# One kernel, a list of new due times, one scaling moved from GpSimd to ScalarE, and three slots with queues of their own

## The chip, the cores and the metric

The kernel runs on one core of a Trainium2 chip. Its engines are TensorE (PE, with its weight loads as PEld), VectorE (DVE), ScalarE (ACT), GpSimd (POOL) and SyncE (SP, which here issues DMAs). The metric is the device time of one execution in microseconds; lower is better.

## The reference

An encoder layer is applied to two sequences, x_prompt and x_sample, each 1024 positions of 1024 features; everything is fp32, and d_ff is 4096. Cut to what matters here:

```
h    = rmsnorm(x, g_mix); proj = h @ w_in
oa   = diff_attention(...)     # 4 heads: softmax 0 minus lam * softmax 1, then @ v
ob   = dilated_mixture(...)    # 8 heads, three patterns of (window, dilation):
                               #   (128,1), (512,4), (2048,16)
  for each pattern: s = q k^T * scale - slope * dist, softmax in the window, o = p @ v, lse
  out  = sum_i softmax_i(lse_i) * o_i
x    = x + concat(norm(oa), norm(ob)) @ w_out
x    = x + square(relu(rmsnorm(x, g_mlp) @ w_up)) @ w_down
y    = rmsnorm(x, g_final)
```

The weights of a dilated head's patterns, softmax over the patterns' denominators, become one factor for each row of probabilities; the kernel multiplies the probabilities by it before they meet v. It joins the three patterns into two sets of scores: bands (dilation 1) and classes (positions with the same remainder modulo 4).

## The kernel before

Each fp32 operand of a large product is split into a rounded high part and the rest, a low part, and three products hi*hi, hi*lo and lo*hi are summed on TensorE. The high part is a cast, mostly on ACT, the low part a subtraction on DVE or POOL. So nearly every product on PE stands behind a pair cast, subtraction.

The work is 16 attention units (8 per sequence; even numbers are two dilated heads, odd ones two differential heads in four tasks), the output projection, and the MLP, whose up and down products use a scheme with 7 instead of 8 block products: it needs sums of weight blocks (`s1` to `s4` in `mlp_up`).

A dilated head m of unit n has two spans. In `a{n}.{m}` (`dil_a`) PE makes 8 blocks of band scores `p1` (128x192 or 128x256) and 8 blocks of class scores `p2` (128x256). DVE adds the bias with a running minimum, ACT takes the exponential. Then the denominators are exchanged between the two layouts by a small permutation product on PE (`cross`, operand `perm`): DVE masks the result into a tile of tag `e`, and reduces it to the factors `dd` (bands) and `f2` (classes). Eight instructions scale `p1` by `dd` and eight scale `p2` by `f2`, all on POOL. In `b{n}.{m}` (`dil_b`) the helper `parts` transposes four 128x128 pieces of the probabilities into PSUM on PE, ACT casts them to the high part (`CAST wt<-psb`), DVE subtracts the low part, and PE multiplies both with v into `pss`. The output goes to a tile `x` of tag `big`.

No loop issues the instructions directly. All work is first recorded into a `Plan`. A table `KEYS` gives each span a start and an end (in units of roughly one attention unit), from which each instruction gets a due time. `Plan.order` then goes through a model of the five engines with its own costs, and on every engine takes the ready instruction that is due first and whose slots are free. Operations with alternatives (`ALT_SUB`, `ALT_MUL`, `ALT_ADD`) go to POOL or DVE, whichever takes them first. `emit` (line 450) issues in that order, so each engine runs a fixed list, in order, and every row of the trace reads L450: rows are told apart by tiles.

Tiles come from tags with a number of slots: `wt` 5 halves of 128x512, `big` 8 of 128x1024, `q` 12. A tag has queues (lanes): within one queue slots are handed out strictly in the order of due times, so a tile that is due earlier and not yet wanted holds up a later one. The changed lines are `q_into` and `k_into` (the scaled q and k before their split, tag `wt`), `dil_a` (the two scalings) and `dil_b` (the tile `x`).

Of the kernel before, what the change touches and what calls it, by code (L numbers as in the profile page):

```python
# [12 lines left out]
F32 = mybir.dt.float32  # L13
# [3 lines left out]
AF = mybir.ActivationFunctionType  # L17
# [29 lines left out]
    "u0": (-4.872, 0.128), "lam": (1.273, 1.359), "a0.0": (0.318, 0.491), "b0.0": (0.695, 0.818),  # L47
    "a0.1": (0.564, 0.959), "b0.1": (0.907, 1.356), "u1": (-0.336, 0.921), "a1.0": (1.16, 1.17),
    "b1.0": (1.384, 1.394), "a1.1": (1.217, 1.476), "b1.1": (1.482, 1.492), "a1.2": (1.521, 2.068),
    "b1.2": (2.062, 2.072), "a1.3": (0.842, 1.209), "b1.3": (1.568, 2.056), "ro1": (2.198, 2.709),  # L50
    "u2": (1.08, 1.998), "a2.0": (1.83, 1.892), "b2.0": (2.698, 2.732), "a2.1": (2.322, 3.199),
    "b2.1": (3.083, 3.202), "u3": (2.615, 2.859), "a3.0": (3.01, 3.22), "b3.0": (3.495, 3.505),
    "a3.1": (3.363, 3.373), "b3.1": (4.079, 4.089), "a3.2": (3.601, 3.727), "b3.2": (4.243, 4.253),
    "a3.3": (3.845, 3.931), "b3.3": (4.137, 4.169), "r1": (2.29, 3.154), "ro3": (3.208, 5.313),
    "u4": (2.996, 3.936), "a4.0": (4.3, 4.31), "b4.0": (4.326, 4.358), "a4.1": (4.269, 5.245),
    "b4.1": (5.263, 5.273), "u5": (4.35, 5.123), "a5.0": (4.877, 5.092), "b5.0": (5.599, 5.609),
    "a5.1": (4.761, 5.876), "b5.1": (5.92, 5.948), "a5.2": (5.207, 5.761), "b5.2": (5.997, 6.117),
    "a5.3": (5.692, 6.054), "b5.3": (6.231, 6.241), "ro5": (6.971, 8.003), "u6": (5.116, 5.981),
    "a6.0": (6.121, 6.131), "b6.0": (6.468, 6.505), "a6.1": (6.434, 6.444), "b6.1": (6.908, 7.14),
    "rg0": (7.977, 8.031), "u7": (5.779, 7.117), "a7.0": (7.1, 7.11), "b7.0": (7.121, 7.486),  # L60
    "a7.1": (7.231, 7.529), "b7.1": (7.554, 7.564), "a7.2": (7.848, 7.912), "b7.2": (8.264, 8.274),
    "a7.3": (7.419, 7.863), "b7.3": (7.608, 8.726), "ro7": (8.492, 8.976), "x": (6.498, 7.176),
    "u8": (7.315, 8.152), "a8.0": (7.997, 8.766), "b8.0": (8.442, 8.775), "a8.1": (8.373, 8.913),
    "b8.1": (9.208, 9.431), "u9": (8.465, 9.183), "a9.0": (8.719, 8.845), "b9.0": (9.936, 9.946),
    "a9.1": (9.591, 10.219), "b9.1": (10.364, 10.437), "a9.2": (8.775, 8.951), "b9.2": (9.497, 9.507),
    "a9.3": (9.562, 9.725), "b9.3": (10.146, 10.156), "ro9": (8.751, 10.698), "u10": (9.24, 10.203),
    "a10.0": (10.545, 10.597), "b10.0": (10.454, 11.086), "a10.1": (10.633, 10.935), "b10.1": (11.156, 11.166),
    "u11": (10.001, 11.039), "a11.0": (10.988, 10.998), "b11.0": (11.337, 12.024), "a11.1": (11.405, 11.602),
    "b11.1": (11.559, 11.916), "a11.2": (12.015, 12.078), "b11.2": (12.033, 12.059), "a11.3": (11.566, 11.916),
    "b11.3": (11.973, 12.339), "ro11": (11.81, 12.373), "u12": (11.182, 11.192), "a12.0": (12.369, 12.493),  # L70
    "b12.0": (12.486, 13.117), "a12.1": (12.219, 12.881), "b12.1": (13.193, 13.415), "u13": (12.244, 12.871),
    "a13.0": (13.077, 13.375), "b13.0": (13.654, 13.692), "a13.1": (13.411, 13.421), "b13.1": (13.693, 13.703),
    "a13.2": (13.806, 13.864), "b13.2": (14.036, 14.124), "a13.3": (13.913, 13.923), "b13.3": (14.122, 14.313),
    "ro13": (13.424, 13.484), "u14": (13.268, 13.612), "a14.0": (14.014, 14.058), "b14.0": (14.617, 14.93),
    "a14.1": (14.123, 14.668), "b14.1": (14.892, 15.12), "rg1": (15.833, 15.876), "u15": (14.405, 15.268),
    "mix": (14.668, 16.212), "a15.0": (15.131, 15.677), "b15.0": (15.493, 16.435), "a15.1": (15.218, 15.531),
    "b15.1": (15.321, 15.634), "a15.2": (15.514, 15.947), "b15.2": (15.799, 16.683), "a15.3": (16.152, 16.411),
    "b15.3": (16.539, 16.638), "ro15": (16.018, 16.028), "out0.0": (15.43, 16.237), "out0.1": (16.478, 17.321),
    "mix0": (16.801, 16.811), "out1.0": (17.313, 17.799), "mix1": (16.996, 17.37), "out1.1": (17.873, 18.085),
    "in0": (17.372, 18.332), "up0.0": (19.76, 19.97), "up0.1": (19.108, 19.877), "as0": (17.468, 19.18),  # L80
    "up0.2": (18.279, 18.585), "up0.3": (19.951, 20.229), "as1": (19.497, 19.731), "up0.4": (20.258, 20.341),
    "up0.5": (20.208, 20.256), "as2": (20.161, 21.47), "up0.6": (22.325, 22.655), "up0.7": (20.453, 22.109),
    "as3": (21.899, 23.125), "up0.8": (22.556, 22.913), "up0.9": (24.937, 25.048), "as4": (20.662, 22.037),
    "up0.10": (23.998, 24.008), "up0.11": (23.047, 23.405), "as5": (22.537, 24.004), "up0.12": (25.576, 25.586),
# [1411 lines left out]
```

## Time and profile before

| | us |
|---|---|
| median of 3 runs | 2608.33 (2605.42 to 2615.72) |
| profiled execution, own time | 2610.55 |
| its span | 2608.4 |
| PE busy | 2523.4 (97%) |
| DVE busy | 1961.3 (75%) |
| ACT busy | 1408.4 (54%) |
| POOL busy | 760.6 (29%) |

Attention takes the span's first 1048 us or so, the output projection's end and the first MLP up product follow at about 1310 us, and the down products end the span. The profile page gives busy time by engine, a coarse picture in 40 slices, the DMA queues, the chain of work that ended last, and groups of instructions by tile. In a timeline row the first number is the start in us from the span's start, the second the length; a bracket says how long the engine had stood idle before and who released it. A row with "x8" is eight instructions back to back.

### The profile page before, as it was taken

The page shows a single profiled execution, that of the slowest core. Times are in us where ns is not written, and L with a number is a line of the kernel's source. Part 1 is how long each engine was busy: PE and PEld are TensorE (multiplying, and loading weights), DVE is VectorE, ACT ScalarE, POOL GpSimd, SP SyncE. Part 2 cuts the span into 40 slices and gives each one's busy share as a digit, 9 for nine tenths or more (in the row PEclk, how much of TensorE's full clock was granted, in tenths as well). Part 3 has the DMA queues.
Part 4 walks back from the last instruction along what each step waited for, and adds up shares of the span by engine and source line. Part 5 has one row for each costly group of instructions (what it writes and reads, how often), then busy time and mean ns, then how long its engine had stood idle before and what let it go on. Part 6 is the DMA issues. An engine that isn't in the chain of part 4 may idle for free. (4 is left out here: it accounts for less than half of the span.)

```text
span 2608.4 us, 36729 instructions
## 1 busy us (share of the span) xinstructions
PE 2523.4 (97%) x12482; PEld 2102.5 (81%) x12482; DVE 1961.3 (75%) x3593; ACT 1408.4 (54%) x2659; POOL 760.6 (29%) x642
## 2 busy tenths in 40 slices
PE   8999999999999999999989999999999999999997
PEld 6888888878888888777777888878887788888877
DVE  7778877897868788887987777557689777545677
ACT  5666665876565757644444444533446545443334
POOL 2305122331223121444342222113243211122464
PEclk9999999999999999999999999999999999999998
DMA  4123121432212121466767666869845444665541
GB/s 163 56 73 112 53 72 47 126 105 67 59 55 75 51 66 56 146 230 220 272 212 256 227 224 231 304 211 357 295 154 177 175 165 136 242 235 198 206 154 65
DMA packets 181402, 412.42 MB, mean 158 GB/s; under 512 B 21344, under 2 KB 27872, under 8 KB 181216
## 3 DMA queue, kind: packets, MB, share of 16 engines
q1 hardware_dynamic: 180640, 409.95, 46.2%
q8 instruction: 98, 1.61, 0.2%
q14 instruction: 88, 0.72, 0.1%
q10 hardware_dynamic: 576, 0.15, 0.0%
HBM read 285.76 MB, written 107.48 MB: 151 GB/s over the span
## 5 line engine op out<-in xcount | busy, mean ns | idle before, releaser
L450 PE MATMUL psb<-h,w 128*128 128x512 f32 x4512 | 1183.7, 400 | 20.0 <-ACT h L450 8.5
L450 PEld LDWEIGHTS psb<-h,w 128*128 128x128 f32 x4512 | 829.0, 190 | 189.7 <-ACT h L450 9.5
L450 PE MATMUL psb<-h 128*128 128x512 f32 (+1 forms) x2448 | 569.9, 383 | 5.3 <-DVE q L450 4.0
L450 PEld LDWEIGHTS psb<-h 128*128 128x128 f32 x2448 | 446.3, 189 | 97.2 <-DVE q L450 2.9
L450 POOL TENSOR_TENSOR w<-w 128x512 fp32r<-128x512 f32 (+1 forms) x127 | 175.0, 1383 | 785.4 <-ACT w L450 659.1
L450 ACT CAST h<-big 128x1024 fp32r<-128x1024 f32 x218 | 220.3, 1051 | 306.2 <-PE psb L450 167.8
L450 DVE TENSOR_TENSOR wt<-psb,wt 128x512 fp32r<-128x512 f32 (+2 forms) x448 | 282.4, 647 | 122.0 <-ACT wt L450 81.0
L450 DVE TENSOR_TENSOR h<-big,h 128x1024 fp32r<-128x1024 f32 x153 | 219.6, 1457 | 125.2 <-ACT h L450 111.5
L450 POOL TENSOR_TENSOR h<-big,h 128x1024 fp32r<-128x1024 f32 x65 | 165.6, 2560 | 384.4 <-ACT h L450 285.6
L450 ACT CAST w<-w 128x512 fp32r<-128x512 f32 x262 | 157.5, 617 | 184.6 <-DMA w<-w_up 95.5
L450 DVE TENSOR_TENSOR w<-w 128x512 fp32r<-128x512 f32 (+1 forms) x233 | 193.7, 836 | 62.1 <-ACT w L450 50.1
L450 PE MATMUL psb<-big,w 128*128 128x512 f32 x768 | 230.2, 394 | 7.1 <-ACT wt L450 7.1
L450 ACT CAST wt<-psb 128x512 fp32r<-128x512 f32 (+2 forms) x288 | 147.6, 538 | 150.1 <-PE psb L450 137.5
L450 PE MATMUL pss<-k,q 128*128 128x512 f32 (+2 forms) x768 | 207.9, 370 | 10.5 <-DVE k L450 4.9
L450 ACT ACTIVATE big<-big,nm 128x1024 f32<-128x1024 f32 x128 | 147.5, 1153 | 66.7 <-DVE nm L450 65.1
L450 PEld LDWEIGHTS psb<-big,w 128*128 128x128 f32 x768 | 145.2, 189 | 39.6 <-ACT wt L450 8.5
L450 PE MATMUL psb<-ident,big 128*128 128x128 f32 (+1 forms) x1032 | 166.2, 273 | 3.2 <-DVE v L450 1.2
L450 DVE CUSTOM_DVE_ANT_0 big<-pss,strip_a 128x1024 f32<-128x1024 f32 x128 | 154.8, 1216 | 10.4 <-PE pss L450 8.6
L450 PEld LDWEIGHTS pss<-k,q 128*128 128x128 f32 x768 | 128.6, 192 | 35.5 <-DVE nm L450 10.4
L450 ACT ACTIVATE wt<-wt 128x512 f32<-128x512 f32 x224 | 133.3, 627 | 37.2 <-DVE wt L450 35.2
L450 ACT ACTIVATE big<-big,s 128x256 f32<-128x256 f32 (+1 forms) x256 | 125.8, 494 | 40.3 <-DVE s L450 40.0
L450 PEld LDWEIGHTS psb<-ident,big 128*128 128x128 f32 (+1 forms) x1032 | 124.0, 140 | 18.5 <-issue 1.6
(184 smaller groups left out, 3429.6 us busy)
## 6 DMA issues: line engine op xcount, KB each, us to landing
ad<-wt SPq DMA_DIRECT2D x218, 256.0 KB, 2.9
big<-ad SPq DMA_DIRECT2D x109, 512.0 KB, 4.5
big<-sd SPq DMA_DIRECT2D x60, 512.0 KB, 4.8
w<-w_in SPq DMA_DIRECT2D x102, 256.0 KB, 3.0
big<-w_down SPq DMA_DIRECT2D x49, 512.0 KB, 4.9
w<-w_up SPq DMA_DIRECT2D x96, 256.0 KB, 4.2
q<-q SPq DMA_DIRECT2D x128, 128.0 KB, 2.3
q<-od SPq DMA_DIRECT2D x64, 256.0 KB, 3.6
```

The source lines that it names most:

```text
L450: getattr(getattr(self.nc, e), m)(**{k: x(v) for k, v in op.kw.items()})
```

## The change

Four edits. The third is on the engine that does it, the second and fourth on which queue a slot is taken from, the first on the order of everything:

```
 KEYS = {                      # all retuned: 198 of 203 pairs have other numbers, for instance
-    "a6.1": (6.434, 6.444), "b6.1": (6.908, 7.14),
+    "a6.1": (6.707, 6.717), "b6.1": (6.933, 6.943),
-    "up0.2": (18.279, 18.585),
+    "up0.2": (18.217, 19.115),
...
     def q_into(q, r):
...
-            t = half("wt")
+            t = half("wt", F32, "e")
...
         k.extend(full("k", F32R) for _ in range(2))
         def evac(_, hf, pb):
-            t = half("wt")
+            t = half("wt", F32, "e")
...
         for b in range(NB):
-            POOL.tensor_scalar(out=p2[b], in0=p2[b], scalar1=f2[:, b // 2, b % 2:b % 2 + 1], scalar2=1.0,
-                               op0=ALU.mult, op1=ALU.mult)
+            ACT.activation(out=p2[b], in_=p2[b], func=AF.Identity, scale=f2[:, b // 2, b % 2:b % 2 + 1])
...
     def dil_b(u, m):
...
-        x = full("big")
+        x = full("big", F32, "x")
```

Over the whole program the issue lists keep PE at 12452 instructions and move the other engines a little: DVE 3595 to 3592, ACT 2281 to 2409, POOL 647 to 522. The 128 instructions from POOL to ACT are 16 heads of 8 scalings. PE rows that carry a wait go from 2249 to 2179; in attention, from 1532 to 1445.

Two places, in the issue lists. The first is the second dilated head of unit u6. On POOL the band scalings (by `dd`) and class scalings (by `f2`) of that head stand in a row before:

```order
L450 TENSOR_SCALAR big_5345<-big_5345,dd_5686 128x192 [waits DVE_49,Activation_49]
L450 TENSOR_SCALAR big_5345<-big_5345,dd_5686 128x256 x3
L450 TENSOR_SCALAR big_5363<-big_5363,dd_5686 128x256 x3
L450 TENSOR_SCALAR big_5363<-big_5363,dd_5686 128x192
L450 TENSOR_SCALAR big_5505<-big_5505,f2_5785 128x256 [waits DVE_49,Pool_49]
L450 TENSOR_SCALAR big_5505<-big_5505,f2_5785 128x256 x3
L450 TENSOR_SCALAR big_5562<-big_5562,f2_5785 128x256 [waits Pool_49]
L450 TENSOR_SCALAR big_5562<-big_5562,f2_5785 128x256 x3
L450 TENSOR_TENSOR q_5432<-q_5432,q_5842 128x512 [waits DMAHW1_49,Activation_49]
```

The class scalings are rows 5 to 8 of these; the next POOL instruction is a norm's product for q. After the change they stand on ACT:

```order
L450 CAST k_5090<-wt_5783 64x512 [waits DVE_49]
L450 ACTIVATE h_5790<-w_5766,g_76 128x512 [waits DMAHW0_49]
L450 ACTIVATE h_5799<-w_5775,g_76 128x512 [waits DMAHW1_49]
L450 CAST k_5091<-wt_5783 64x512
L450 CAST wt_5794<-psb_5793 128x512 [waits PE_49]
L450 ACTIVATE q_5779<-q_5779 128x512 [waits DMAHW2_49]
L450 ACTIVATE big_5589<-big_5589,f2_5834 128x256 [waits DVE_49]
L450 ACTIVATE big_5589<-big_5589,f2_5834 128x256 x3
L450 ACTIVATE big_5615<-big_5615,f2_5834 128x256 x4
L450 CAST wt_5813<-psb_5812 128x512 [waits PE_49,Activation_49]
L450 ACTIVATE h_5863<-w_5824,g_76 128x512 [waits DMAHW3_49]
L450 ACTIVATE big_5663,l0_5869<-big_5663,nm_5857 128x1024 [waits DVE_49]
```

The last of the eight is directly in front of `CAST wt_5813<-psb_5812`, a high part of that head's transposed probabilities. On PE this part of the list reads, after the change:

```order
L450 MATMUL psb_5820<-e_5810,perm1_74 128x32 [waits DVE_49]
L450 MATMUL psb_5812<-ident_68,big_5543 128x128 [waits Pool_49]
L450 MATMUL pss_5662<-k_5090,q_4990 128x512 [waits DVE_49,Activation_49]
L450 MATMUL pss_5662<-k_5090,q_4991 128x512
L450 MATMUL pss_5802<-k_5090,q_4990 128x512
L450 MATMUL pss_5802<-k_5090,q_4991 128x512
L450 MATMUL pss_5866<-wt_5794,v_4466 128x256 [waits DVE_49,Activation_49]
L450 MATMUL pss_5866<-wt_5795,v_4466 128x256
L450 MATMUL pss_5866<-wt_5794,v_4466 128x256
L450 MATMUL pss_5866<-wt_5795,v_4466 128x256
L450 MATMUL pss_5866<-wt_5813,v_4466 128x256 [waits Activation_49]
L450 MATMUL psb_5876<-ident_68,big_5543 128x128
```

The first row is the permutation product whose result becomes `f2`; the product that needs `wt_5813` is the eleventh. Before, 18 rows lie between the same two, among them products of the input projection (`psb<-h,w`) and eight transposes; the last eleven of the list there are:

```order
L450 MATMUL psb_5721<-h_315,w_5691 128x512
L450 MATMUL psb_5721<-h_338,w_5680 128x512
L450 MATMUL psb_5748<-ident_68,q_5178 128x128
L450 MATMUL psb_5721<-h_338,w_5680 128x512
L450 MATMUL psb_5721<-h_338,w_5691 128x512
L450 MATMUL psb_5797<-ident_68,big_5345 128x128 [waits DVE_49]
L450 MATMUL psb_5797<-ident_68,big_5345 128x128 [waits Pool_49]
L450 MATMUL psb_5797<-ident_68,big_5345 128x128
L450 MATMUL psb_5797<-ident_68,big_5363 128x128 [waits Pool_49]
L450 MATMUL psb_5748<-ident_68,q_5178 128x128 x2
L450 MATMUL pss_5812<-wt_5778,v_4470 128x256 [waits Activation_49]
```

The last is the product that needs the first high part of that head's transposed probabilities; the projection's products that stood between have gone elsewhere in the list.

The second place is on DVE where the output projection ends and the first MLP product begins. Before, from the last sum of the third of four quarters (`strip_a<-psb`) on:

```order
L450 TENSOR_TENSOR strip_a_14379<-psb_14389,strip_a_14379 128x512 [waits DMAHW1_49,DMAHW0_49,PE_49]
L450 TENSOR_TENSOR h_14447<-w_14177,h_14447 128x512 [waits Activation_49]
L450 SCALAR_TENSOR_TENSOR w_14429<-w_14429,g_76,w_13830 128x512 [waits DMAHW4_49,DVE_49]
L450 TENSOR_TENSOR h_14459<-w_14261,h_14459 128x512 [waits Activation_49]
L450 TENSOR_TENSOR h_14466<-w_14287,h_14466 128x512 [waits Activation_49]
L450 TENSOR_TENSOR w_14347<-w_14429,w_14347 128x512 [waits DVE_49]
L450 TENSOR_TENSOR q_14488<-w_14429,big_14394 128x512 [waits Activation_49]
L450 SCALAR_TENSOR_TENSOR w_14464<-w_14464,g_76,w_13830 128x512 [waits DMAHW0_49]
L450 TENSOR_TENSOR strip_b_14434<-psb_14441,strip_b_14434 128x512 [waits DMAHW5_49,DMAHW2_49,PE_49]
```

```order
L450 TENSOR_TENSOR h_14490<-w_14347,h_14490 128x512 [waits Activation_49]
L450 SCALAR_TENSOR_TENSOR w_14478<-w_14478,g_76,w_13830 128x512 [waits DMAHW1_49]
L450 TENSOR_TENSOR strip_a_14509<-w_14425,w_14438 128x512 [waits DMAHW7_49,DMAHW6_49,DMAHW3_49]
L450 TENSOR_TENSOR w_14464<-w_14478,w_14464 128x512 [waits DVE_49]
L450 TENSOR_TENSOR q_14516<-w_14478,big_14511 128x512 [waits Activation_49]
L450 TENSOR_TENSOR w_14520<-w_14425,w_14476 128x512
L450 TENSOR_TENSOR h_14518<-w_14464,h_14518 128x512 [waits Activation_49]
L450 SCALAR_TENSOR_TENSOR w_14484<-w_14484,g_76,w_13830 128x512 [waits DMAHW2_49]
L450 SCALAR_TENSOR_TENSOR w_14496<-w_14496,g_76,w_13830 128x512 [waits DMAHW3_49]
L450 TENSOR_TENSOR w_14438<-w_14438,strip_b_14514 128x512 [waits DMAHW5_49]
L450 TENSOR_TENSOR w_14484<-w_14496,w_14484 128x512 [waits DVE_49]
L450 TENSOR_TENSOR w_14425<-w_14438,w_14425 128x512 [waits DVE_49]
```

`w_14520` is the low part of the first block of w_up that PE multiplies, `w_14425` in the last row the sum `s2` for its second product, and `strip_b<-psb` the last quarter's sum, on which the norm and so the MLP's input wait. After:

```order
L450 TENSOR_TENSOR strip_a_14370<-psb_14379,strip_a_14370 128x512 [waits DMAHW5_49,DMAHW4_49,PE_49]
L450 SCALAR_TENSOR_TENSOR w_14409<-w_14409,g_76,w_13863 128x512 [waits DMAHW7_49]
L450 TENSOR_TENSOR h_14438<-w_14217,h_14438 128x512 [waits Activation_49]
L450 TENSOR_TENSOR w_14334<-w_14409,w_14334 128x512 [waits DVE_49]
L450 TENSOR_TENSOR h_14450<-w_14270,h_14450 128x512 [waits Activation_49]
L450 TENSOR_TENSOR h_14455<-w_14301,h_14455 128x512 [waits Activation_49]
L450 TENSOR_TENSOR h_14468<-w_14334,h_14468 128x512 [waits Activation_49]
L450 TENSOR_TENSOR strip_a_14483<-w_14415,w_14424 128x512 [waits DMAHW4_49,DMAHW2_49,DMAHW0_49]
L450 TENSOR_TENSOR w_14491<-w_14415,w_14463 128x512 [waits DVE_49]
L450 TENSOR_TENSOR strip_b_14419<-psb_14429,strip_b_14419 128x512 [waits DMAHW6_49,DMAHW1_49,PE_49]
```

```order
L450 SCALAR_TENSOR_TENSOR w_14460<-w_14460,g_76,w_13863 128x512 [waits DMAHW5_49]
L450 SCALAR_TENSOR_TENSOR w_14473<-w_14473,g_76,w_13863 128x512 [waits DMAHW6_49]
L450 SCALAR_TENSOR_TENSOR w_14480<-w_14480,g_76,w_13863 128x512 [waits DMAHW7_49]
L450 TENSOR_TENSOR w_14460<-w_14473,w_14460 128x512 [waits DVE_49]
L450 TENSOR_TENSOR q_14524<-w_14473,big_14519 128x512 [waits Activation_49]
L450 SCALAR_TENSOR_TENSOR w_14486<-w_14486,g_76,w_13863 128x512 [waits DMAHW0_49]
L450 TENSOR_TENSOR h_14526<-w_14460,h_14526 128x512 [waits Activation_49]
L450 TENSOR_TENSOR w_14480<-w_14486,w_14480 128x512 [waits DVE_49]
L450 TENSOR_TENSOR w_14424<-w_14424,strip_b_14521 128x512 [waits DMAHW3_49]
L450 TENSOR_TENSOR q_14535<-w_14486,big_14519 128x512 [waits Activation_49]
L450 TENSOR_TENSOR h_14533<-w_14480,h_14533 128x512 [waits Activation_49]
L450 TENSOR_TENSOR w_14415<-w_14424,w_14415 128x512 [waits DVE_49]
```

The same three are `w_14491`, `w_14415` (last row) and `strip_b<-psb`. Counted from `strip_a<-psb`, the low part moves from 14 rows behind it to 8, and so in front of `strip_b<-psb`, which goes from 8 to 9, and the sum `s2` from 20 to 22.

## Rows read from the trace of the kernel before

**Rows 1.** The page's first part: span, busy time of each engine.

```profile
span 2608.4 us, 36729 instructions
...
PE 2523.4 (97%) x12482; PEld 2102.5 (81%) x12482; DVE 1961.3 (75%) x3593; ACT 1408.4 (54%) x2659; POOL 760.6 (29%) x642
```

**Rows 2.** Windows: stretch, length, busy time by engine, PE clock, DMA.

```profile
core 0: us, PE busy (x) PEld busy (x) DVE busy (x) ACT busy (x) POOL busy (x), PEclk, DMA share, GB/s
0.00:1048.00 1048.00, 1017.48 (x5702) 870.62 (x5702) 825.65 (x2041) 681.31 (x1533) 269.26 (x352) 1.00 0.26 77
1048.00:1430.00 382.00, 357.33 (x1667) 288.35 (x1666) 316.24 (x493) 188.28 (x337) 151.71 (x104) 0.97 0.65 225
```

**Rows 3.** Waits of PE, first 1100 us: total us, times, longest.

```profile
PE psb L450 <- ACT h L450: 8.5, 2, 7.9
PE pss L450 <- DVE k L450: 4.9, 5, 2.7
PE pss L450 <- DVE nm L450: 4.5, 4, 2.6
PE psb L450 <- DVE wt L450: 4.0, 7, 1.1
PE psb L450 <- DVE v L450: 2.8, 4, 1.2
```

**Rows 4.** Instructions by line and shape: busy, mean ns | idle before.

```profile
L450 ACT CAST wt<-psb 128x512 fp32r<-128x512 f32 x240 | 135.5, 585 | 131.6 <-PE psb L450 120.1 <-issue 4.4 <-POOL w L450 4.0
...
L450 POOL TENSOR_SCALAR big<-big,f 128x256 f32<-128x256 f32 x128 | 68.0, 551 | 2.8 <-DVE f L450 1.3 <-PE psb L450 1.1 <-DVE rs L450 0.2
...
L450 ACT ACTIVATE v<-v,g 128x256 f32<-128x256 f32 x8 | 3.7, 498 | 0.1
```

**Rows 5.** Timeline, 1024.5 to 1034 us: from permutation product to class scalings.

```profile
1025.61 0.30 PE L450 MATMUL psb<-e,perm 128*128 128x32 f32 x2
...
1025.95 0.19 DVE L450 TENSOR_TENSOR e<-psb,sel 128x32 f32<-128x32 f32 x1
...
1026.40 0.20 DVE L450 TENSOR_REDUCE f<-e 128x8 f32<-128x32 f32 x1
...
1026.77 3.66 POOL L450 TENSOR_SCALAR big<-big,f 128x256 f32<-128x256 f32 x8 [1.29 <-DVE f L450]
```

**Rows 6.** Timeline, 2585 to 2592 us: ACT scaling at the class blocks' shape.

```profile
2589.38 1.29 ACT L450 ACTIVATE v<-v,g 128x256 f32<-128x256 f32 x3
```

**Rows 7.** Timeline, 902.5 to 911 us: scalings beside DVE, cast before PE.

```profile
905.14 4.96 POOL L450 TENSOR_SCALAR big<-big,f 128x256 f32<-128x256 f32 x8
...
905.54 1.96 DVE L450 TENSOR_TENSOR q<-wt,q 64x512 fp32r<-64x512 f32 x2 [0.19 <-ACT q L450]
...
906.18 0.59 ACT L450 CAST wt<-psb 128x512 fp32r<-128x512 f32 x1
...
906.82 0.19 PEld L450 LDWEIGHTS pss<-wt,v 128*128 128x128 f32 x1 [0.19 <-ACT wt L450]
```

**Rows 8.** Timeline, 238 to 246 us: the same subtraction with POOL idle.

```profile
240.75 1.40 DVE L450 TENSOR_TENSOR k<-wt,k 64x512 fp32r<-64x512 f32 x2 [0.69 <-ACT k L450]
...
244.24 1.29 POOL L450 TENSOR_TENSOR q<-q 128x512 f32<-128x512 f32 x1 [5.66 <-ACT q L450]
```

**Rows 9.** Timeline, 1306 to 1318 us: PE's pace in the output projection.

```profile
1305.82 12.40 PE L450 MATMUL psb<-h,w 128*128 128x512 f32 x54
```

**Rows 10.** Timeline, 1316 to 1327 us: the first product of the MLP.

```profile
1320.31 0.67 DVE L450 TENSOR_TENSOR strip_b<-psb,strip_b 128x512 f32<-128x512 f32 x1
...
1323.98 0.67 DVE L450 TENSOR_TENSOR w<-w 128x512 fp32r<-128x512 f32 x1
...
1324.71 1.22 PE L450 MATMUL psb<-v,w 128*128 128x512 f32 x2 [5.34 <-DVE w L450]
```

**Rows 11.** Timeline, 1327 to 1337 us: its second product.

```profile
1331.11 0.73 PE L450 MATMUL psb<-h,w 128*128 128x512 f32 x2 [1.77 <-ACT w L450]
```

**Rows 12.** Windows: the first product's own stretch.

```profile
1324.70:1331.00 6.30, 4.63 (x10) 3.14 (x10) 5.75 (x8) 2.19 (x5) 1.70 (x1) 0.62 0.17 63
```

104 rows, old and new, of the table KEYS are left out of this document.

## The prediction

> **What bounds the kernel now.** The page's first part comes first: PE is busy 2523.4 of 2608.4 us, DVE three quarters of the span, ACT half and POOL under a third [rows 1]. So a change that adds no work to PE can win at most PE's idle time, 2608.4 - 2523.4 = 85.0 us, and only by ending waits of PE; work taken from POOL is worth nothing by itself. The windows say where that idle time lies: in attention, 1048.0 - 1017.48 = 30.5 us; from there to the end of the first up products, 382.0 - 357.33 = 24.7 us [rows 2]. The waits of PE say for whom it waits in attention. One wait at the start, 7.9 us for ACT's `h`, is out of reach of these edits; of the rest the four largest groups, 4.9 + 4.5 + 4.0 + 2.8 = 16.2 us, all name DVE, in pieces of 1 to 3 us, and none names POOL [rows 3]. The timelines then give the prices below.
>
> PE runs its list in order, so what counts for an edit is how much PE work lies in the list between the last PE instruction that a needed result depends on and the PE instruction that needs it. I call that the cover. At full clock 54 matmuls of 512 columns took 12.40 us, so one is worth 0.23 us of cover [rows 9], and by its columns I take half of that for 256.
>
> **The scaling.** Eight scalings took POOL 3.66 us, 0.46 each [rows 5]; on ACT three scalings of the same shape by a factor per row took 1.29 [rows 6]. One by itself takes 0.498 [rows 4], so the starts are (1.29 - 0.50) / 2 = 0.40 apart, and eight block ACT for 3.2 us. Over 16 heads that is 128 x 0.40 = 51 us more on ACT. In attention ACT had 681.31 of 1048 us [rows 2] and then has 732, 70%: as a whole it does not become the bound.
>
> A rule of the Trainium skill speaks against moving this at all: GPSIMD Engine Reference, section 4.1 Engine selection, says that elementwise work with one input runs on GpSimd at roughly line rate. The rows agree, 0.46 against 0.40. By that rule the edit gains only what POOL's being freed gains.
>
> What it costs is position. ACT takes its list in order, and in 13 of the 16 heads the instruction directly behind the eight scalings is a `CAST wt<-psb`, which PE waits for. From the permutation product the chain is: 0.99 us to the end of the `f` reduction (1025.61 to 1026.60) and 0.17 to the engine that scales [rows 5], 3.2 for the eight, 0.59 for the cast and 0.05 until PE loads the weights (906.18 + 0.59 = 906.77, then 906.82) [rows 7]. Sum 5.0 us. On POOL that chain ended nowhere near PE's next need.
>
> Against 5.0 stands the cover in the new PE list, head by head in order: 2.2, 5.1, 6.1, 5.9, 4.7, 7.2, 4.5, 1.5, 1.8, 4.8, 2.4, 11.9, 4.3, 4.4, 6.5, 5.6 us. The heads with 2.2, 1.8, 2.4 and 5.6 have their scalings not in one block but with other ACT work and the casts among them, so I count nothing there. The others that fall short: 0.3, 0.5, 3.5, 0.2, 0.7 and 0.6, together **+5.8 us**. The 3.5 is the second head of u6, the place shown: behind the permutation product there is one transpose, four score products of 512 and four of 256 columns, 1.5 us in all. The upper bound counts the interleaved heads too, 2.8 + 3.2 + 2.6 more, +14.4; the lower is 0, if DVE or the slots delay PE there anyway.
>
> **Port relief.** The same two DVE subtractions took 1.40 us with POOL idle [rows 8] and 1.96 while POOL scaled `big` by `f` [rows 7]: 0.56 us of DVE per head's block, 16 x 0.56 = 9 us of DVE time that the edit gives back. About half of what PE waits for in attention names DVE (16.2 of 30.5 us) [rows 2, 3], so I take half of 9: **-4.5 us**. Bounds: 0, if those subtractions have cover; -16.2, if every wait in rows 3 that names DVE goes.
>
> The Trainium skill is harsher here: SBUF — State Buffer, section SBUF: two separate sides, calls the port pair of VectorE and GpSimd an exclusive lock, held for a whole instruction, with the other engine blocked. The trace agrees in part: DVE was stretched from 1.40 to 1.96 beside POOL, not stopped for all of POOL's 4.96 us [rows 7, 8]. Taken as said, 68.0 us of POOL's scalings [rows 4] would be 68 us in which such DVE work was held; that is what rival B below makes of DVE's waits.
>
> **The queues.** `e` and `x` change which tile is handed a slot first, not how many slots there are. They act through the order alone and I price them with it. What they could gain is a q or k that no longer stands behind a due `wt` pair; what they could cost is a `wt` slot fewer for the pairs that PE waits for.
>
> **The order.** Outside the two places shown I compare how close PE stands to its inputs. In attention the list has 106 products with under 1 us of cover before and 87 after; 30.5 us of idle time over 106 is 0.29 each, so 19 fewer are worth **-5.5 us**. That this is soft is seen by a wider count: products with under 1.3 us of cover go from 175 to 188. Bounds: -15, half of attention's idle time [rows 2], and +12, as much again as a fifth more short products than counted (0.29 x 40).
>
> At the end of the output projection the DVE list changes hands. Before, PE waits 5.34 us for the low part of the first w_up block [rows 10] and, after ten products, another 1.77 for the second product's weights [rows 11]. DVE's instructions start about 0.61 apart there (six from 1320.31 to 1323.98) [rows 10]. The low part now stands six rows sooner: 6 x 0.61 = 3.7 us, the first wait falls to 1.7. But the sum `s2` for the second product is two rows later, 1.2 us, and PE gets there 3.7 sooner: the second wait grows to 1.77 + 3.7 + 1.2 = 6.7. Together **+1.2 us**: one wait is cut and handed to the next. Bounds -1 (if DVE's list runs tighter behind the low part) and +2. The slow clock stays where a long wait is: the ten products after the 5.34 us stand at a granted clock of 0.62, 4.63 us for ten [rows 12] against 2.3 at full rate; a wait of 6.7 will have the same behind it, so I count that neither way.
>
> The rest, the down products and the tail, is issued almost in the old order; zero.
>
> **Sum.** +5.8 - 4.5 - 5.5 + 1.2 = -3.0 us, against the profiled execution's own 2610.55, which is 2.2 above the median of the runs: 2607.5, and in terms of the median 2605.3. **Forecast 2605 us**; its own terms move it between about 2595 and 2615.
>
> **Rivals.**
>
> B, DVE's waits go. If POOL's scalings are what delays DVE in attention, the 16.2 us go whole; if also ACT's blocks turn out covered (0 for 5.8): 2608.3 - 16.2 - 5.5 + 1.2 = 2588. For it: all the larger groups of waits in attention name DVE, in short pieces [rows 3]. Against: they name k, nm, wt and v, which stand everywhere, while the scalings by `f` fill 68 of 1048 us [rows 2, 4].
>
> C, slower: ACT's block is late at most heads. If something of 1.2 us stands between f's end and the first scaling (an exponential of 128x1024, or the cast of q or k, is about that long), the chain is 6.2 us, not 5.0. Then the covers above, the interleaved heads now counted too, fall short by 4.0, 1.1, 0.1, 0.3, 1.5, 0, 1.7, 4.7, 4.4, 1.4, 3.8, 0, 1.9, 1.8, 0 and 0.6: 27.3 us. 2608.3 + 27.3 - 4.5 - 5.5 + 1.2 = 2627. It decides from a chain of about 5.7 us on, at which the loss passes 20 us, or if the casts of q and k queued behind the block stop PE as well. For it: 131.6 us in which ACT stood idle before those casts were almost all spent waiting for PE [rows 4], that is, ACT now takes a cast the moment it is there, and no longer would. Against: twelve heads have over 4 us of cover, and the block is only 3.2.
>
> D, nothing moves: the class scalings are covered on either engine, the slots were free, the short products that vanish were no waits. 2608.
>
> **How the numbers follow.** Of a measurement of this kernel I call 0.5% no change: 2595.3 to 2621.4. Chances: forecast 0.45, D 0.13, B 0.25, C 0.17. The forecast gives 0.07 to faster and 0.01 to slower, B 0.24 to faster and 0.01 to the same, C 0.15 to slower and 0.02 to the same, D all to the same: faster 0.31, same 0.53, slower 0.16. The range leaves a tenth at each side, half of B below 2588 and half of C above 2625: 2586 to 2625.
>
> **What would show it.** In the new trace, the second head of u6: eight `ACTIVATE big<-big,f2` in 3.2 us, the cast behind them, and a wait of PE of about 3.5 us for it. If PE shows no wait there, the chain or the cover is misread. The total of PE's waits in attention on ACT's `wt` should be near 6 us, that on DVE below 16.2; if the DVE waits keep their size, port relief is worth nothing. At the first up product, waits of about 1.7 and 6.7 us. POOL's busy time should be some 68 us smaller and ACT's some 50 larger. What would make the prediction wrong is a new long wait at a place that I priced at zero: the down products, the tail, or a slot of `wt` that q and k now take first.

## The result, and the profile after

The changed kernel takes 2633.95 us (median of 4 runs, 2627.91 to 2635.33), the kernel before 2606.88 beside it: the medians lie 27 us apart. The ratio over all their executions is 1.0092, with a 95% interval of 1.0078 to 1.0105, some 24 us slower; 2605 and a small gain were forecast, and the range ended at 2625.

The page's first part after the change, to be read against [rows 1]:

```profile
span 2633.2 us, 36660 instructions
...
PE 2529.0 (96%) x12482; PEld 2104.7 (80%) x12482; DVE 1947.8 (74%) x3590; ACT 1452.3 (55%) x2787; POOL 673.2 (26%) x517
```

The work moved as the diff says: POOL 87 us less, ACT 44 more (some 68 and 50 were forecast), PE's instructions the same. PE is busy 5.6 us longer for the same work and idle 104.2 us instead of 85.0, so 19 of the 25 us are idle time. The same two windows as in [rows 2], after the change:

```profile
core 0: us, PE busy (x) PEld busy (x) DVE busy (x) ACT busy (x) POOL busy (x), PEclk, DMA share, GB/s
0.00:1048.00 1048.00, 1013.89 (x5669) 868.00 (x5670) 808.66 (x2016) 721.24 (x1641) 214.84 (x240) 0.99 0.25 77
1048.00:1430.00 382.00, 347.43 (x1621) 280.10 (x1620) 309.45 (x482) 186.28 (x339) 138.37 (x93) 0.96 0.61 210
```

In 1048 us PE gets through 33 instructions fewer than before, in the next 382 us through 46 fewer. Windows at fixed times drift apart like that, so the comparison that carries the rest is made at equal work. Each PE instruction of a trace is given a weight, the 30th percentile of the time from its start to the next start among instructions of its tiles in the trace of before; the weights are summed up along PE's list, and the times at which two traces reach the same sum are subtracted. The table is worked out so from the traces: how far each kernel is behind the kernel before, in us, when before is at the time on top.

```
before at (us)     500    580   1060   1180   1330   1440   1640   1970   2080   2590
changed kernel    -1.3    5.3    4.9    7.0   18.3   21.3   36.2   34.8   24.8   24.9
frozen_act         6.6    8.4   14.6   14.8   15.8   15.0   14.3   15.5   12.7   11.7
frozen_pool        5.1   11.6   16.4   14.7   22.8   26.6   39.3   38.8   27.3   27.2
attn_new          -1.9    4.6    4.0    4.1   11.9   11.0   11.0   10.9    7.4    6.8
attn_old          10.5   15.1   21.5   18.7   24.8   28.6   46.7   45.7   35.4   36.1
up_old            -3.0    3.1    2.6    2.9   16.4   20.1   22.9   21.3   11.0   11.1
out_old           -4.3    2.4    1.8    5.2    4.9   14.5   29.0   27.9   18.5   21.0
lanes              5.2    5.8    7.4    6.6    5.2    7.2   10.0   10.0    7.3    6.5
only_up            5.7    6.3    7.6    5.7    2.5   11.9   27.7   27.7   24.1   23.9
copy_first        -2.0    5.1    4.4    4.5   13.3   18.5   34.3   33.1   24.5   25.6
stores_act        -2.0    5.0    4.3    8.2   16.7   19.3   34.5   32.9   23.7   26.2
sums_first        -2.2    4.0    3.5    5.4   14.2   28.3   44.2   42.8   32.8   33.2
stores_later      -2.0    5.2    4.6    5.4   14.8   21.1   45.7   44.1   34.0   36.6
```

Of the changed kernel it says: attention ends 5 us late, all of it lost at the second head of u6 (500 to 580); 16 us go between 1060 and 1440, the end of the output projection and the first up products; 15 more in the other up products of the first sequence (1440 to 1640); 10 come back by 2080. The 10 come back only where the due times behind the first sequence are the new ones (8.6 to 11.5 us between 1970 and 2080 in those rows; 2.7 to 3.6 in frozen_act, attn_new, lanes and only_up), in a stretch in which PE of the kernel before stands idle for some 8.6 us: there the new list wins. One caution: copy_first, stores_act, sums_first and stores_later have the changed kernel's lists unaltered up to about 1340, and stand at 13.3 to 16.7 there against its 18.3. So up to 5 us of that column is what one execution differs from the next.

The three places that the prediction named. The second head of u6 in the timeline (start, length, engine, what; idle before it):

```profile
519.48 0.47 PE L450 MATMUL psb<-e,perm 128*128 128x32 f32 x2
...
522.07 2.45 DVE L450 SCALAR_TENSOR_TENSOR h<-w,g,h 128x512 fp32r<-128x512 f32 x2
522.18 3.30 ACT L450 ACTIVATE big<-big,f 128x256 f32<-128x256 f32 x8 [0.29 <-DVE f L450]
524.55 1.40 DVE L450 TENSOR_TENSOR k<-wt,k 64x512 fp32r<-64x512 f32 x2
525.38 2.05 PE L450 MATMUL pss<-k,q 128*128 128x512 f32 x4 [5.16 <-DVE k L450]
525.39 0.56 ACT L450 CAST wt<-psb 128x512 fp32r<-128x512 f32 x1
```

Eight scalings take 3.30 us (3.2 were worked out from [rows 4, 6]), and the cast stands behind them. But PE is stopped one product sooner, for a subtraction of k which on DVE stands behind two products of `h` with the norm's gain: 5.16 us, not the 3.5 of the cast.

The first up product:

```profile
1336.56 0.50 PE L450 MATMUL psb<-v,w 128*128 128x512 f32 x1 [1.45 <-ACT w L450]
...
1340.24 1.22 PE L450 MATMUL psb<-v,w 128*128 128x512 f32 x2 [2.95 <-DVE w L450]
...
1351.83 1.22 PE L450 MATMUL psb<-h,w 128*128 128x512 f32 x2 [6.96 <-ACT w L450]
```

The waits of 5.34 and 1.77 [rows 10, 11] have become 2.95 and 6.96 (1.7 and 6.7 were forecast, from places in DVE's list; in the list after the change one row, a `q<-w,big`, stands between the two parts shown, and with it `s2` is the 22nd, as counted), with one of 1.45 in front that was not. Ahead of it, in the output projection, stands a wait that the prediction had no term for; the longest there before was 3.36 us (at 1272 us):

```profile
1258.55 2.08 PE L450 MATMUL psb<-h,w 128*128 128x512 f32 x4 [5.80 <-DVE w L450]
```

The other up products, PE's waits by what released them (total, times, longest), first the kernel before from 1330 to 1690 us, then the changed one from 1355 to 1705:

```profile
PE psb L450 <- ACT wt L450: 3.0, 1, 3.0
PE psb L450 <- ACT w L450: 1.8, 1, 1.8
PE pss L450 <- ACT h L450: 1.7, 1, 1.7
```

```profile
PE psb L450 <- ACT wt L450: 8.1, 6, 1.8
PE psb L450 <- ACT w L450: 3.2, 4, 1.4
PE psb L450 <- POOL w L450: 1.6, 2, 0.8
```

Six waits for ACT's `wt`, each for the copy of the first product's sum; the single one before was for another instruction, at 1387 us. The waits grow by some 7 us, half of the 15. What the rest is shows in two stretches of equal work (PE busy, its instructions and so on as in [rows 2]), first before, then changed:

```profile
1440.00:1630.00 190.00, 189.52 (x831) 155.43 (x829) 142.74 (x190) 91.29 (x161) 49.57 (x33) 1.00 0.65 226
```

```profile
1465.00:1670.00 205.00, 193.95 (x828) 155.03 (x827) 137.82 (x185) 89.94 (x161) 57.30 (x37) 0.99 0.62 218
```

PE is idle 11 us instead of 0.5, and busy 4 us longer. The prediction had no term for this place.

### The profile page after: what moved, and what is told of

Same layout as the page of the kernel before. It is cut to its first block, busy times and chain, and to the rows that moved or that the text cites. A ratio compares the mean times of both kernels' runs of the same rounds, so it can differ in the third digit from the quotient of the medians.

```text
span 2633.2 us, 36660 instructions
## 1 busy us (share of the span) xinstructions
PE 2529.0 (96%) x12482; PEld 2104.7 (80%) x12482; DVE 1947.8 (74%) x3590; ACT 1452.3 (55%) x2787; POOL 673.2 (26%) x517
## 5 line engine op out<-in xcount | busy, mean ns | idle before, releaser
L450 POOL TENSOR_TENSOR w<-w 128x512 fp32r<-128x512 f32 (+1 forms) x116 | 157.6, 1362 | 658.4 <-ACT w L450 489.5
L450 DVE TENSOR_TENSOR w<-w 128x512 fp32r<-128x512 f32 (+1 forms) x244 | 206.0, 848 | 78.4 <-ACT w L450 61.6
L450 POOL TENSOR_TENSOR h<-big,h 128x1024 fp32r<-128x1024 f32 x52 | 132.8, 2562 | 427.3 <-ACT h L450 355.7
L450 PE MATMUL pss<-k,q 128*128 128x512 f32 (+2 forms) x768 | 200.8, 369 | 13.6 <-DVE nm L450 7.2
```

The lines of the kernel that those rows point to most:

```text
L450: getattr(getattr(self.nc, e), m)(**{k: x(v) for k, v in op.kw.items()})
```

## The experiments

**Which edit, and where.** Theory A: the loss is in the re-dealt order behind attention; the moved scaling costs little. Theory B, rival C of the prediction: ACT, blocked by the scalings, is late for PE. The first two runs hold an issue order fixed, row for row, and change only the scalings' engine as each instruction is issued.

frozen_act, on the kernel before:

```
+ if e == "gpsimd" and m == "tensor_scalar" and scalar1 is a tile f2:
+     e, m, kw = "scalar", "activation", dict(..., func=AF.Identity, scale=scalar1)
```

> The kernel before with its own issue order kept row for row; only the 128 class scalings are issued on ScalarE at the same place of the order. Theory A (the loss is in the re-dealt order behind 1090 us, the moved scaling costs little): 2607 to 2615 us, up to 8 us above before, PE waits on ScalarE's wt in attention up by at most 8 us. Theory B (ScalarE blocked by the scalings is late for PE and the delay is passed on): 2620 us or more.

Measured 1.0053 (1.0035 to 1.0071), median 2625: in theory B's range, but at some 13 us only half of what the changed kernel loses. PE's waits in the first 1100 us:

```profile
PE psb L453 <- ACT h L453: 8.5, 2, 7.8
PE pss L453 <- ACT wt L453: 8.2, 14, 1.4
PE psb L453 <- DVE wt L453: 4.2, 8, 1.1
PE pss L453 <- DVE k L453: 4.0, 5, 2.0
PE psb L453 <- DVE v L453: 3.0, 4, 1.1
PE psb L453 <- DVE k L453: 1.9, 3, 0.8
PE pss L453 <- DVE nm L453: 1.8, 3, 1.0
```

This is rival C's mechanism at work: 14 waits for ACT's `wt` at the dilated heads' products `pss<-wt,v`, 8.2 us, where the kernel before has one of 0.3. `k`, `nm`, `wt` and `v` of [rows 3] come to 13.0 us instead of 16.2, but that this is port relief isn't shown: DVE's first 2044 instructions, the same in both lists, last 937.0 us in sum instead of 938.6 (worked out from the traces), and a PE that is held up elsewhere comes later to its other inputs. At the old order the edit costs 14.6 us of attention; these waits are 8.2 of them.

frozen_pool is the reverse on the changed kernel's order (the same lines with the engines exchanged).

> The changed kernel with its own issue order kept row for row; only the 128 class scalings go back to GpSimd at the same place of the order. Theory A: 2627 to 2637 us, the loss stays. Theory B: 2615 us or less, the loss is gone.

1.0109 (1.0092 to 1.0125): no relief, which speaks against theory B. In the table attention gets 11.5 us worse (16.4 against 4.9), of which 2.3 are left at the end (27.2 against 24.9). Here DVE does feel POOL's scalings: its first 2017 instructions, the same in both lists, last 927.8 us instead of 919.6. So each order suits the engine that it was made with, and the scaling's engine is not what loses the 24 us.

attn_new and attn_old split the table of due times: `KEYS` new for the attention spans and old behind, and the other way round.

> The changed code with the new due times for the attention spans alone, the old ones from the output projection on. Theory A: the loss up to 1060 us (5 us) and a part of what lies between 1090 and 1250 us stay, 2610 to 2620 us. Theory B: 2625 us or more, since all scalings on ScalarE and all attention due times are as in the changed kernel.

> The changed code with the old due times for the attention spans, the new ones from the output projection on. Theory A: the loss behind 1250 us stays, 2620 to 2632 us. Theory B: the scalings stay on ScalarE but stand elsewhere; 2607 to 2618 us if the attention due times put them where they hurt.

attn_new 1.0025 (1.0010 to 1.0039), median 2617, within theory A's range; attn_old 1.0120 (1.0098 to 1.0143), median 2645, above the ranges of both. Most of the loss goes with the due times behind attention; with the scalings on ACT and the old due times, attention alone loses 21.5.

One limit of all runs that change `KEYS`: the order is made anew, so more than the named spans moves. PE's list parts from the changed kernel's at 1075 us in attn_new and out_old and at 1107 in up_old, and only_up's from lanes' at 1131.

**Which due times behind attention.** A1: those of the up products. A2: those of the output projection and the entry into the MLP.

```
 KEYS:  up_old   old pairs for up0.0 .. up0.15, as0 .. as7
        out_old  old pairs for out0.*, out1.*, mix0, mix1, in0
        only_up  new pairs for up0.*, as* alone, in the kernel `lanes`
```

> The changed kernel with the old due times for the spans of the first sequence's up products and the sums of w_down beside them; all else as changed. Theory A1 (of the loss behind 1250 us most is made in the list of the up products themselves): 2614 to 2624 us, and the six waits of PE on ScalarE's wt between 1480 and 1680 us are gone. Theory A2 (it is made before, where the output projection ends, and the up products only follow): 2628 us or more.

> The changed kernel with the old due times for the output projection, the mix and the entry into the MLP alone. Theory A1: 2628 us or more, 0 to 6 us gained. Theory A2: 2610 to 2622 us.

up_old 1.0042 (1.0027 to 1.0057), out_old 1.0084 (1.0069 to 1.0099). In the table up_old loses 3 us between 1440 and 1640 instead of 15, and of the six waits for the copy one of 0.28 us is left. out_old is 13 us better at 1330 and has given all but 7 back by 1640: what is won at the entry is lost in the up products again. That is A1 for the 15 us. The loss between 1180 and 1330 isn't settled by these runs: up_old has it (13.5 us), attn_new with the old due times has 7.8, out_old with the same ones has none.

lanes is the kernel before with the three queues alone:

```
-            t = half("wt")            # q_into, k_into
+            t = half("wt", F32, "e")
-        x = full("big")
+        x = full("big", F32, "x")
```

> The kernel before with the own queues of the three slots alone; old due times, class scalings on GpSimd. If the queues only act through the due times: 2602 to 2614 us, within 0.3% of before. If letting scaled q and k take wt slots first costs the pairs that PE waits for: 2618 us or more.

1.0020 (1.0010 to 1.0031). Small, but not nothing: the queues alter the order and attention ends 7.4 us late in the trace.

> As lanes (class scalings on GpSimd, own queues, old due times; ratio 1.0020), but with the new due times of the first sequence's up products and the sums beside them. If these due times are enough for their part of the loss: 1.005 to 1.008 of before, all of the growth between 1400 and 1700 us. If they only hurt together with what stands ahead of them: 1.001 to 1.004.

1.0076 (1.0058 to 1.0093): on top of lanes, 15 us by the ratios and 17.4 in the traces, where the table puts 20 between 1330 and 1640, 7 of them before 1440. So the new due times of the up products are enough by themselves, with the scalings on POOL and old due times everywhere else. They do it by other waits, though: from 1380 to 1700 us PE waits 5.8 us for DVE's `w` in three places and 4.1 for ACT's `wt` in two.

**By which list they do it.** In the changed kernel PE waits for ACT's copy; in front of it on ACT stand squares and casts; these wait for DVE's sums; in front of those on DVE stand the next block's weight sums, which wait for loads. DVE's waits, the changed kernel from 1465 to 1670 us:

```profile
DVE w L450 <- ACT w L450: 27.9, 21, 4.8
DVE strip_a L450 <- DMA w<-w_up: 11.3, 4, 4.6
DVE w L450 <- POOL w L450: 7.9, 5, 3.5
DVE w L450 <- POOL strip_a L450: 6.8, 3, 3.1
DVE wt L450 <- PE psb L450: 5.8, 8, 1.9
```

and the kernel before, 1440 to 1630:

```profile
DVE w L450 <- ACT w L450: 22.6, 18, 2.9
DVE wt L450 <- PE psb L450: 12.7, 11, 3.4
DVE w L450 <- POOL w L450: 4.8, 5, 1.8
DVE wt L450 <- ACT wt L450: 3.6, 5, 1.4
DVE strip_a L450 <- DMA w<-w_up: 1.9, 2, 1.0
```

DVE waits for loads of w_up 11.3 us instead of 1.9, and for PE 5.8 instead of 12.7. (In only_up the wait for these loads is 4.9 us, so it is not needed for a loss of that size.) Four runs each altered one list of the changed kernel in the up products and left the rest as it was:

```
copy_first    ACT:  COPY wt<-psb taken directly behind the product it reads
stores_act    SP:   ad<-wt of what ACT squared is issued on ACT's queue
sums_first    DVE:  wt<-psb,wt taken directly behind the product it reads
stores_later  SP:   ad<-wt, sd<-v directly in front of w<-w_up taken behind it
```

> The changed kernel with its order, but in the first sequence's up products ScalarE's copy of the first block's sum is taken directly behind the product it reads, instead of behind up to three other ScalarE instructions. If the queue in front of that copy is what PE waits for: the six waits of 8.1 us fall to 2 or less and the time by 5 to 8 us, to 2626 to 2629. If PE is late for another reason there (VectorE, slots), 2631 us or more.

> The changed kernel and order; in the first sequence's up products the stores of what ScalarE has just squared are issued on ScalarE's queue, so SyncE's queue of weight loads no longer stands behind them. If late loads behind stores feed the lateness (VectorE then waits for a load in front of the sums, ScalarE for the sums, SyncE for ScalarE): VectorE's waits on loads of w_up between 1465 and 1670 us fall from 11.3 us to under 5, PE's waits on ScalarE's wt go, and the time falls by 7 to 13 us against the changed kernel. If the loads are late for want of slots: within 3 us, or slower by ScalarE's issues.

> The changed kernel and order; in the first sequence's up products each VectorE sum of a block product is taken directly behind the product it reads, in front of the next block's weight sums. If those weight sums in front (they wait 11.3 us for loads and 18 us for POOL there) are the cause: PE's waits on ScalarE's wt between 1480 and 1680 us fall from 8.1 us to 3 or less and the time by 5 to 12 us. If the weights' sums are themselves what PE needs next, the waits only move to DVE's or ACT's w and the time stays within 4 us.

> The changed kernel and order; on SyncE's list alone, in the first sequence's up products, stores that stand directly in front of a load of w_up are taken behind it. If stores in front make the loads late: VectorE's waits on loads of w_up between 1465 and 1670 us fall below 5 us and the time falls by 7 to 13 us against the changed kernel, to a ratio of 1.004 to 1.006 to before. If the loads are late because their slots are handed out late: ratio 1.008 or more.

Measured 1.0112 (1.0095 to 1.0129), 1.0084 (1.0066 to 1.0103), 1.0119 (1.0096 to 1.0143) and 1.0128 (1.0110 to 1.0146): against the changed kernel's 1.0092 (1.0078 to 1.0105) none gains and all four expectations of a gain failed; stores_later loses clear of the noise, copy_first and sums_first lie higher with intervals that overlap. In copy_first PE's waits for ACT's `wt` only fall from 8.1 to 5.3 us; the copy stands further in front, but ACT's list still waits for DVE ahead of it (timeline from 1555 us):

```profile
1554.78 0.63 ACT L460 ACTIVATE wt<-wt 128x512 f32<-128x512 f32 x1 [2.93 <-DVE wt L460]
...
1555.82 0.58 ACT L460 COPY wt<-psb 128x512 f32<-128x512 f32 x1
...
1556.45 3.02 PE L460 MATMUL psb<-big,w 128*128 128x512 f32 x12 [2.66 <-ACT wt L460]
```

In stores_act DVE waits for the same loads for 11.6 us. sums_first, PE's waits from 1340 to 1720 us:

```profile
PE psb L469 <- ACT w L469: 19.9, 7, 7.0
PE psb L469 <- ACT wt L469: 5.3, 4, 2.2
```

With the sums in front, the weights are late instead. stores_later cuts DVE's waits for loads to 4.8 us (1465 to 1680 us), and DVE waits 14.1 us for stores instead, which now hold the slots of its sums:

```profile
DVE w L486 <- ACT w L486: 27.8, 20, 4.3
DVE wt L486 <- DMA ad<-wt: 14.1, 6, 4.2
...
DVE strip_a L486 <- DMA w<-w_up: 4.8, 3, 1.7
```

So the lateness isn't one list's. My reading, which no run tests as a whole, is that loads, weight sums, product sums, copies and stores form a loop through the slots, in which the next one is late whichever is put first. Which due time in that table opens the gap stays open.

**The heads and the clock.**

frozen_act_cf (frozen_act, with casts taken in front of the class scalings that stand ahead of them):

> As frozen_act (order of before kept, class scalings on ScalarE), but each cast of transposed probabilities that stands behind class scalings is taken in front of them. If the casts behind the block are what costs in frozen_act (13 us): 2607 to 2614 us, and the waits of PE pss<-wt,v at the heads go. If ScalarE's 51 us of more work costs through other rows (exponentials, k and q casts): 2619 us or more.

1.0049 (1.0034 to 1.0065), against 1.0053: a miss. PE's waits for ACT's `wt` at `pss` are 8.8 us instead of 8.2. That these casts stand behind the block isn't the whole of it; what else on ACT is late for them wasn't settled.

u6_fix (changed kernel; at the second head of u6 the two k subtractions and the cast are taken directly behind what they read):

> The changed kernel and order; only at the second head of u6 VectorE's two subtractions for k and ScalarE's cast behind the class scalings are taken directly behind what they read. If the position in those lists is the 8 us lost there: PE's waits of 5.16 and 0.57 us fall to 2 in sum or less, the time by 3 to 5 us against the changed kernel. If PE was late there by POOL's band scalings anyway: within 1 us of the changed kernel.

1.0072 (1.0057 to 1.0087). The wait for k goes, but the next one takes its place; from 505 to 560 us:

```profile
PE pss L475 <- ACT big L475: 2.4, 1, 2.4
PE pss L475 <- DVE big L475: 2.4, 1, 2.4
PE psb L475 <- POOL big L475: 2.1, 1, 2.1
```

At 580 us it is 2 us ahead of the changed kernel, less than the 3 to 5 expected; the rest of its gain lies where executions differ.

a11_before (kernel before; the fourth block of the first up product in a slot of its own):

```
-        a11 = fetch(1, 1, half("strip_b"))
+        a11 = fetch(1, 1, half("wt") if not s and c == 2 else half("strip_b"))
```

> The kernel before; only in the first up product the fourth block of w_up is loaded into a slot of wt instead of strip_b, which the last quarter of the output projection holds until it is stored. If that load is what sets the second product's sum: the wait of 1.77 us goes, 1 to 2 us faster than before. If VectorE's list position sets it: same wait, within 1 us.

1.0007 (0.9997 to 1.0016): no change in time, but not the same wait either. The second wait is gone:

```profile
1325.02 1.22 PE L450 MATMUL psb<-v,w 128*128 128x512 f32 x2 [8.53 <-DVE w L450]
...
1329.45 3.31 PE L450 MATMUL psb<-h,w 128*128 128x512 f32 x12
```

The first wait is longer because PE comes to it 2.9 us sooner in this execution; it ends at 1325.0, against 1324.7 before. The second product starts 1.7 us sooner, and by 1440 us the two kernels are level again. DVE's list changes too, from 1324 us on, so whether the slot or the list took the wait away isn't shown; no time came of it.

The waits at u6 have the clock at its lower level behind them. Windows, the changed kernel, then warm_u6:

```profile
519.30:533.00 13.70, 7.98 (x31) 6.60 (x30) 11.37 (x18) 10.15 (x22) 3.57 (x5) 0.50 0.46 172
```

```profile
519.30:533.00 13.70, 11.73 (x90) 10.48 (x91) 12.67 (x23) 12.08 (x25) 2.59 (x4) 1.00 0.38 132
```

warm_u6 and attn_new_warm keep PE busy there, with 18 and 45 transposes of the identity in front of the two waiting products (`PE.transpose(out=unread, in_=ident, identity=ident)`), in the changed kernel and in attn_new:

> The changed kernel and order; at the second head of u6 PE gets 18 and 45 transposes of the identity in front of the two products that wait there (2.2 and 5.2 us), written where nothing reads them. If the clock at its lower level for 13.7 us behind those waits is a cost of its own: the clock stays at 1.00 there and the time falls by 6 to 10 us against the changed kernel, to a ratio of about 1.006 to before. If only the waits cost: within 1 us, or slower by what the filling overshoots.

> As warm_u6, on the version with the new due times in attention and the old ones behind (attn_new, ratio 1.0025 to before). Clock as a cost of its own: 6 to 9 us less, 0.999 to 1.000 of before. Waits alone: 1.002 to 1.003.

The granted clock stays at 1.00 instead of 0.50, 2.4 instead of 1.2 GHz. warm_u6 measured 1.0061 (1.0042 to 1.0080), attn_new_warm 1.0022 (1.0010 to 1.0034) against attn_new's 1.0025. At 580 us warm_u6 is 2.8 us behind before (changed kernel 5.3) and attn_new_warm 2.9 (attn_new 4.6). So 13.7 us at half clock cost about 2 (2.5 and 1.7 in these traces): in them PE is busy for 7.98 us and DVE for 11.37. The rest of warm_u6's gain isn't repeated in attn_new_warm.

No version beat the kernel before.

## Why the prediction was wrong

The step that failed is "The rest, the down products and the tail, is issued almost in the old order; zero". It left out the up products of the first sequence behind the first one altogether: 15 us between 1440 and 1640, shown by up_old (the loss goes with their due times) and only_up (these alone bring a loss of that size). The prediction priced places where PE waited before, and showed no stretch behind 1430 us [rows 2]. A stretch in which PE had hardly waited (idle 0.5 us in 190) was taken for safe. The zero was wrong behind it too, where 11 us come back, mostly between 1970 and 2080.

By stage, forecast against table: attention -4.2 and 4.9; from there to 1440 us 1.2 and 16.4; from 1440 to 1640 0 and 14.9; behind that 0 and -11.3. The second of these is the other step that failed: it was priced as two waits of one product.

Point by point:

- The scaling, +5.8 us by the casts' cover. The chain was right (3.30 us for eight), and the head that was named, the second of u6, is where attention loses its 5 us. The releaser was not: DVE's k stopped PE one product sooner, and u6_fix shows a further one behind. PE's waits for ACT's `wt` in the first 1100 us come to 5.7 us, near the 6 forecast, but by luck: 5.5 are at `psb<-wt,v`, products of the differential heads, and 0.2 at the dilated heads. At a fixed order the same edit costs 14.6 us (frozen_act), 8.2 of it in waits for these casts; so rival C's mechanism exists, and the new due times avoid it.
- Port relief, -4.5. The four groups of [rows 3] keep their size, 16.9 us instead of 16.2, so by the prediction's own sign it was worth nothing to PE. The 9 us of DVE time behind it depend on the order: 1.5 us in the old one (frozen_act), 8.2 in the new (frozen_pool against the changed kernel).
- The order in attention, -5.5 by counting short products. The sign was right and the size wrong: with scalings on ACT and own queues, attention ends 21.5 us late with the old due times (attn_old) and 4.9 with the new, so these are worth 16.6. They make up for most of what the scalings (14.6, frozen_act) and the queues (7.4, lanes) cost in the old order; the three give 5.4. That the count of short products measures such a gain isn't shown; the wider count pointed the other way.
- The queues, priced with the order. lanes shows 0.20% by itself, 7 us in attention, against nothing forecast.
- The first up product, +1.2. The mechanism and both sizes came out, roughly: 2.95 and 6.96 for 1.7 and 6.7; with the 1.45 us in front the waits there sum to 11.4 instead of 7.1. But it was judged alone. Between 1060 and 1440 us the kernel falls 16 us behind, up to 5 of them the execution's own, with the wait of 5.80 in the output projection among them; which due times make that loss stays open. out_old shows that a gain at the entry doesn't last.
- Rival C's time, 2627, came nearest, for the wrong place: that is luck. B is excluded (attention doesn't gain), D too.

## What to carry to other kernels

Where a table of due times is changed as a whole, price every stretch in which PE runs without waits, not only the places where it waits now: here such a stretch lost 15 us. An edit and the order around it are one thing: by the end of attention the same move of the scalings to ACT costs 14.6 us in the old order and saves 11.5 in the new. A saving in one stage can be gone later: of the 11.5, 2.3 are left at the end. Where loads, sums, copies and stores share few slots and are late, four runs that each moved one of them in its list gained nothing.

## What the runs showed of the hardware

A lower granted clock need not cost its share: 13.7 us at 0.50 cost about 2 us. PE was busy for 7.98 of them; that it waited for other engines through the rest is the likely reason, not a tested one. And POOL's two-input work stops a DVE instruction with two inputs from SBUF much longer than its scalings by a factor do. In the changed kernel:

```profile
1139.49 2.74 POOL L450 TENSOR_TENSOR v<-v 128x1024 f32<-128x1024 f32 x1
...
1139.95 2.83 DVE L450 TENSOR_TENSOR h<-q,h 128x512 fp32r<-128x512 f32 x1
```

The same DVE form takes 0.68 us at 1258.49 us, and ends here 0.55 us after POOL does. Of 17 such subtractions of 128x512 in that trace that started while a two-input POOL instruction ran, 12 were stretched, to between 0.82 and 2.83 us, and all 12 ended 0.55 or 0.56 us after it; the other five took 0.68, and the 59 with no POOL work beside them took 0.68 or 0.69. Beside POOL's scalings two subtractions only went from 1.40 to 1.96 us [rows 7, 8]. Over the kernel before, subtractions of that kind (64x512) take 0.69 us in the mean with POOL idle, 0.83 beside its scalings and 1.14 beside its two-input work.

SBUF — State Buffer, section SBUF: two separate sides, of the Trainium skill calls the shared port an exclusive lock held for a whole instruction: the row above agrees with it. So do the rows beside the scalings: there the instruction that holds the port is one scaling (4.96 us for eight, 0.62 each), and the two subtractions lost 0.56 together. The prediction had taken the eight for one.
